# A hybrid encoder layer with a dense PEER stage: the building of the gate matrix tied to u tiles, VectorE making the low parts, and top-k positions compared in pairs

## The chip, the cores and the metric

The kernel runs on one core of a Trainium2 chip. The metric is the device time of the whole kernel in microseconds; the median of three runs stands for it. Its engines are PE (TensorE), DVE (VectorE), ACT (ScalarE), POOL (GpSimd) and SP (SyncE, which here only issues transfers). SPq and ACTq in a row are the transfer queues that SP and ACT issue. All matrix products of the big stages take 32-bit numbers as a high part `hi` (rounded) and a low part `lo` (the rest), as three products hi·hi, lo·hi, hi·lo.

## What is computed

The layer has 512 tokens of width 1024 (and 16 meta tokens in the first half). Its first half, attention, a gated linear recurrence and their projection, is not touched. The second half is PEER: each token picks, for each of 8 heads, 16 of 128·128 single-neuron experts by two lists of 128 keys.

```python
q = (xi @ w_q).reshape(n, PEER_HEADS, 2, PEER_KEY_DIM)
s = jnp.einsum('nhpc,hpkc->nhpk', q, sub_keys)
ts, ti = lax.top_k(s, PEER_TOPK)                      # 16 of 128, for each of the two lists
cand_s = ts[:, :, 0, :, None] + ts[:, :, 1, None, :]  # 256 sums
cand_i = ti[:, :, 0, :, None] * PEER_NKEYS + ti[:, :, 1, None, :]
best_s, best_p = lax.top_k(cand_s, PEER_TOPK)         # the 16 best pairs
idx = jnp.take_along_axis(cand_i, best_p, axis=-1)
gate = jax.nn.softmax(best_s, axis=-1)
act = jax.nn.gelu(jnp.einsum('nd,nhkd->nhk', xi, u[idx]), approximate=False)
return jnp.einsum('nhk,nhkd->nd', (gate * act), v[idx])
```

## The kernel before

The 512 tokens are four tiles t = 0 to 3 of 128. For t = 1 to 3 (384 tokens) PEER is computed densely: for each of 128 tiles of 128 experts a **u tile** gives gelu(u·x) for all 384 tokens, a matrix W holds each token's gates (zero where an expert was not picked), and a **v tile** adds (W·gelu)·v into the output. For t = 0 it is done sparsely: 256 indirect transfers on POOL (`gather`, L251) fetch rows of u and v, and DVE uses them (L265, L263).

The second half runs in these stages.

- **Scores and top 16.** PE multiplies by w_q and the keys; DVE takes the 16 best of 128 (`top16`, L183 to L187). `topk2` (L192 to L243) is the work behind it for half the heads and two token tiles: 80 candidate sums, their 16 best, the positions split into a row and a column number `rf` and `cf`, and then the key numbers by comparing each position with 0 to 15 (L231), multiplying with the list `tf` (L233) and folding 16 terms to one (L234 to L237). An Exp on ACT and a division (L240 to L243) give the gates. It runs four times; the last two are the list `late`.
- **u phase** (the first `LA` = 60 u tiles). A u tile loads `raw` (SP, L108, two buffers), makes `hi` on ACT (L114) and `lo` on POOL (L116; on DVE for tiles from 60 on), then 24 matmuls (L127 to L129), a gelu on ACT (L1055), and a spill to memory, `A_d` (L1057, issued by ACT). Beside it `wbuild` makes W. For a token tile, PE transposes the gates and the two key numbers (`sel`, L974) and ACT copies them out; then, for 8 tokens at a time (a step; 48 steps), DVE compares the two key numbers with `ioh` (L993, twice), multiplies the first one-hot by the gates' low part `gl` (L994) and high part `gh` (L996; every fourth step ACT does the latter, L999), PE multiplies (L1021, L1022: 8 matmuls for a bank of 4 tokens, two banks in a step), ACT copies the bank into `stg` (L1024), and every four steps SP writes `stg` to memory, `W_d` (L1026). I call the banks W0 to W95 and the tiles U0 to U127, V0 to V127. Sixteen gathers of u rows are issued in this phase (`RA` = 0.4 for each u tile).
- **v phase.** 128 v tiles with 18 matmuls each (L1080 to L1084) and, from U59 on, the remaining u tiles between them, whose gelu is not spilled. SP loads W and the spilled gelus four tiles at a time (`wa`, L1111 and L1113), and `vraw`. The other gathers are issued here.

The order of each engine's queue is set when the program is built, by a scheduler that follows a simulated timeline; the program's own order and explicit dependencies (`add_manual_dep`) steer it. In the main loop `wbuild` is advanced by a budget: after u tile i it may have used the share (i + 1)/(LA − ET − 1) of the whole cost, with a guessed cost for each piece (3.0, 4.0, 2.2 behind `yield`).

Ahead of the u phase, the tile `iof` (the numbers 0 to 127, from which `ioh` is made, L949 and L950) lies in memory that the stage before has to leave first.

Of the kernel before, what the change touches and what calls it, by code (L numbers as in the profile page):

```python
# [9 lines left out]
F32 = mybir.dt.float32  # L10
# [14 lines left out]
P = 128  # L25
# [24 lines left out]
SC = 16  # L50
# [29 lines left out]
PU = 100  # L80


def _emit(ctx, tc, I, out):
# [71 lines left out]
    io16 = cst.tile([P, TOPK], F32, name="io16")  # L155

# [32 lines left out]
    def topk2(a, b, sm, cand, tf, eq, zs):  # L189
        ts_ = tsv[:, b, 2 * a:2 * a + 2].rearrange("p t h c r -> p (t h) c r")  # L190
        ti_ = tiv[:, b, 2 * a:2 * a + 2].rearrange("p t h c r -> p (t h) c r")
        nc.vector.tensor_copy(tf, ti_)  # L192
# [25 lines left out]
        cf = sm("cf")  # L218
        nc.vector.tensor_copy(rf, row)
# [141 lines left out]
    nc.sync.dma_start(out=io16, in_=I["iota"][:, :TOPK].to_broadcast([P, TOPK]))  # L361
    ropc = fx("ropc", [P, TM], "ropc")
# [532 lines left out]

    keys = qs.tile([P, 2 * PH, NK], F32, name="keys")
# [371 lines left out]
```

## Time and profile before

| what | us |
|---|---|
| median of three runs | 1678.58 (1675.06 to 1680.83) |
| profiled run, its own time | 1682.47 |
| span of the profiled run | 1680.7 |
| first matmul of U0 | 466.21 |
| first matmul of W0 | 566.74 |
| end of the last matmul of W95 | 814.2 |
| first matmul of V0 | 846.18 |

In the page's list of busy time PE has 1574.4 us (94% of the span), DVE 1291.4 (77%), ACT 739.6 (44%), POOL 677.1 (40%). These shares are means over stages with different limits: between 500 and 850 us, which is where the u phase lies, PE is idle for about a sixth of the time. A row of the waits says for whom an engine sat idle before an instruction, for how long in total, how often, and the longest.

### The profile page before, as it was taken

The page shows a single profiled execution, that of the slowest core. Times are in us where ns is not written, and L with a number is a line of the kernel's source. Part 1 is how long each engine was busy: PE and PEld are TensorE (multiplying, and loading weights), DVE is VectorE, ACT ScalarE, POOL GpSimd, SP SyncE. Part 2 cuts the span into 40 slices and gives each one's busy share as a digit, 9 for nine tenths or more (in the row PEclk, how much of TensorE's full clock was granted, in tenths as well). Part 3 has the DMA queues.
Part 4 walks back from the last instruction along what each step waited for, and adds up shares of the span by engine and source line. Part 5 has one row for each costly group of instructions (what it writes and reads, how often), then busy time and mean ns, then how long its engine had stood idle before and what let it go on. Part 6 is the DMA issues. An engine that isn't in the chain of part 4 may idle for free.

```text
span 1680.7 us, 24243 instructions
## 1 busy us (share of the span) xinstructions
PE 1574.4 (94%) x8793; PEld 1392.4 (83%) x8793; DVE 1291.4 (77%) x2529; ACT 739.6 (44%) x1229; POOL 677.1 (40%) x465
## 2 busy tenths in 40 slices
PE   6999998989986789979989999999999999999998
PEld 6888886768876689878978888889999999988996
DVE  3888768647999998948247777778887888778777
ACT  5454555543324474867533333333333333333334
POOL 3443112076334467475411212154545444344442
PEclk9999999989997989999999999999999999999999
DMA  6112222232224557656999999899999998999885
GB/s 232 54 46 81 69 61 69 84 118 89 78 73 149 176 193 250 239 218 252 328 366 342 326 314 326 278 313 389 321 329 326 336 327 315 319 339 327 308 276 185
DMA packets 152360, 387.42 MB, mean 231 GB/s; under 512 B 12752, under 2 KB 71376, under 8 KB 150576
## 3 DMA queue, kind: packets, MB, share of 16 engines
q1 hardware_dynamic: 106160, 238.79, 41.2%
q0 software_dynamic: 36864, 134.23, 22.8%
q10 hardware_dynamic: 9216, 12.85, 2.1%
q8 instruction: 69, 1.13, 0.3%
q14 instruction: 51, 0.42, 0.1%
HBM read 342.56 MB, written 40.63 MB: 228 GB/s over the span
## 4 chain that ended last, share of the span: by engine, by line
PE 28%; issue 18%; DVE 12%; POOL 10%; DMA 6%; ACT 3%; SPq 1%; POOLq 0%; ACTq 0%; DVEq 0%
POOL gat L251 7%; PE banka L1080 4%; PE banka L1083 4%; PE banka L1084 4%; POOL lo L116 3%; PE bankp L1080 2%; PE bankp L1083 2%; PE bankp L1084 2%; PE bankg L129 2%; DMA gat<-v,idx 2%; PE bankg L127 2%; PE bankg L128 2%; DMA raw<-uT 2%; DVE oh L993 2%; DMA gat<-u,idx 1%
## 5 line engine op out<-in xcount | busy, mean ns | idle before, releaser
L116 POOL TENSOR_TENSOR lo<-raw,hi 128x1024 fp32r<-128x1024 f32 x81 | 238.4, 2947 | 228.8 <-ACT hi L114 220.4
L114 ACT CAST hi<-raw 128x1024 fp32r<-128x1024 f32 x177 | 185.8, 1051 | 289.6 <-PE bankg L128 159.1
L127 PE MATMUL bankg<-un_hi,hi 128*128 128x384 f32 x880 | 300.1, 341 | 12.2 <-ACT act L1055 12.2
L129 PE MATMUL bankg<-un_hi,lo 128*128 128x384 f32 x880 | 299.6, 341 | 5.3 <-POOL lo L116 5.2
L128 PE MATMUL bankg<-un_lo,hi 128*128 128x384 f32 x880 | 297.9, 338 | 0.0
L251 POOL DMA_INDIRECT gat<-u,idx x128 | 157.8, 1232 | 299.5 <-PE bankp L1084 252.1
L251 POOL DMA_INDIRECT gat<-v,idx x128 | 167.8, 1311 | 207.6 <-PE bankp L1084 180.4
L263 DVE SCALAR_TENSOR_TENSOR acc<-gat,sact,acc 128x1024 f32<-128x1024 f32 x128 | 164.2, 1283 | 72.2 <-DMA gat<-v,idx 61.6
L265 DVE CUSTOM_DVE_ANT_0 gat<-gat,hn 128x1024 f32<-128x1024 f32 x128 | 162.9, 1282 | 53.2 <-DMA gat<-u,idx 53.1
L127 PEld LDWEIGHTS bankg<-un_hi,hi 128*128 128x128 f32 x880 | 168.1, 191 | 16.1 <-ACT act L1055 12.5
L135 DVE TENSOR_TENSOR vhl<-vraw,vhl 128x1024 fp32r<-128x1024 f32 x128 | 157.1, 1228 | 30.9 <-ACT vhl L134 30.8
L129 PEld LDWEIGHTS bankg<-un_hi,lo 128*128 128x128 f32 x880 | 167.9, 191 | 8.1 <-POOL lo L116 6.8
L128 PEld LDWEIGHTS bankg<-un_lo,hi 128*128 128x128 f32 x880 | 167.7, 191 | 3.4
L134 ACT CAST vhl<-vraw 128x1024 fp32r<-128x1024 f32 x128 | 134.2, 1049 | 46.3 <-PE bankp L1084 33.4
L116 DVE TENSOR_TENSOR lo<-raw,hi 128x1024 fp32r<-128x1024 f32 x96 | 117.8, 1228 | 24.2 <-ACT hi L114 23.0
L1024 ACT ACTIVATE stg<-banka 128x512 f32<-128x512 f32 x96 | 96.2, 1140 | 1.7 <-PE banka L1022 0.9
L993 DVE TENSOR_TENSOR oh<-iT,ioh 128x1024 f16<-128x1024 f16 x96 | 80.8, 888 | 2.4 <-PE banka L1022 2.4
L1021 PE MATMUL banka<-oh 128*128 128x128 f16 x384 | 55.3, 233 | 22.1 <-DVE oh L996 12.7
L1055 ACT ACTIVATE act<-bankg 128x384 f32<-128x384 f32 x110 | 53.4, 486 | 23.2 <-PE bankg L129 12.1
L1021 PEld LDWEIGHTS <-oh 128*128 128x128 f16 x384 | 39.2, 104 | 20.8 <-DVE oh L996 15.0
L1022 PE MATMUL banka<-oh 128*128 128x128 f16 x384 | 54.3, 233 | 0.7 <-DVE oh L994 0.7
L129 PE MATMUL bankp<-un_hi,lo 128*128 128x384 f32 x144 | 48.7, 338 | 4.5 <-POOL lo L116 4.5
(2283 smaller groups left out, 3906.3 us busy)
## 6 DMA issues: line engine op xcount, KB each, us to landing
raw<-uT SPq DMA_DIRECT2D x128, 512.0 KB
vraw<-v SPq DMA_DIRECT2D x128, 512.0 KB
W_d<-stg SPq DMA_DIRECT2D x12, 2048.0 KB
wa<-W_d SPq DMA_DIRECT2D x32, 768.0 KB
A_d<-act ACTq DMA_DIRECT2D x60, 192.0 KB
wa<-A_d SPq DMA_DIRECT2D x15, 768.0 KB
raw<-wq SPq DMA_DIRECT2D x16, 512.0 KB
raw<-win_n SPq DMA_DIRECT2D x12, 512.0 KB
```

The source lines that it names most:

```text
L114: nc.scalar.copy(hi, raw)
L116: (eng or nc.vector).tensor_sub(lo, raw, hi.bitcast(F32))
L127: nc.tensor.matmul(o, lhsT=ah, rhs=bh, start=start, stop=False)
L128: nc.tensor.matmul(o, lhsT=ah, rhs=bl, start=False, stop=False)
L129: return nc.tensor.matmul(o, lhsT=al, rhs=bh, start=False, stop=stop)
L134: last[0] = nc.scalar.copy(hi, src).ins.name
L135: (eng or nc.vector).tensor_sub(lo, src, hi.bitcast(F32))
L251: g = nc.gpsimd.indirect_dma_start(out=r, out_offset=None, in_=src, in_offset=bass.IndirectOffsetOnAxis(ap=idx[:, hk:hk + 1], axis=0))
L263: nc.vector.scalar_tensor_tensor(acc0, r, sact[:, hk:hk + 1], acc0, op0=ALU.mult, op1=ALU.add)
L265: nc.vector.tensor_tensor_reduce(r, r, hn0, scale=1.0, scalar=0.0, op0=ALU.mult, op1=ALU.add, accum_out=sact[:, hk:hk + 1])
L993: nc.vector.tensor_tensor(o12[:, j], tok(iT[:, j]), ioh[:, None, :, :].to_broadcast(sh), op=ALU.is_equal)
L1080: m0 = nc.tensor.matmul(o, lhsT=gh_[:, tc_], rhs=vh[:, dc], start=(j == 0), stop=False, skip_group_check=True)
```

## The change

1. **W is tied to u tiles.** The budget is gone. Step n of `wbuild` belongs to u tile `tgt(n)` = 15 + int(0.48·n), 10 more from n = 14 on; the first matmul of a step and the transposes are tied (order only) behind the last matmul of that u tile. The steps of t = 1 without the last two start at U15, the rest at U31.
2. **Gates later.** `topk2` no longer ends with Exp and division; they are the function `fin`, called for two at a time, its Exp tied behind the gelu of u tile 13 and of u tile 30.
3. **Low parts on VectorE.** `LP` = 8: POOL makes `lo` for U0 to U7 only; DVE makes it for the rest.
4. **Pairs.** Positions `rb`, `cb` are bf16; `tf` and the numbers 0 to 15 (`io16b`) hold each entry twice, so that two positions lie side by side and every operand of the comparison is 16 bits wide with adjacent elements. The fold has 3 adds and a last one for each list, as before.
5. **One-hots in one piece.** The two comparisons of a step are one instruction on 128x2048; the two multiplications also, except in each fourth step.
6. `iof` has a place of its own and is loaded ahead of the keys.
7. `W_d` is written from ACT's queue instead of SP's.
8. `RA` 0.4 → 0.15 (5 gathers in the u phase in place of 16), `LA` 60 → 56 (4 u tiles move into the v phase), `SC` 16 → 14 (buffers of the scores).

```diff
-SC = 16
+SC = 14
-RA = 0.4
+RA = 0.15
-LA = 60
+LA = 56
-PU = 100
+LP = 8
+A0 = 15
+AR = 0.48
+AG = 10
+AL = 14
...
-        nc.vector.tensor_copy(tf, ti_)
+        nc.vector.tensor_copy(tf, ti_[:, :, :, :, None].to_broadcast([P, PH, 2, TOPK, 2]))
...
-        for j, pos in enumerate((rf, cf)):
-            nc.vector.tensor_tensor(eq, pos[:, :, :, None].to_broadcast([P, PH, TOPK, TOPK]),
-                                    io16[:, None, None, :].to_broadcast([P, PH, TOPK, TOPK]), op=ALU.is_equal)
...
-        nc.scalar.activation(gate, gate, AF.Exp)
...
+        for j, pos in enumerate((rb, cb)):
+            e4 = eq
+            nc.vector.tensor_tensor(e4.rearrange("p g (r q) -> p g r q", q=2),
+                                    pos.rearrange("p h (s q) -> p (h s) q", q=2)[:, :, None, :].to_broadcast([P, PH * 8, TOPK, 2]),
+                                    io16b[:, None].to_broadcast([P, PH * 8, TOPK, 2]), op=ALU.is_equal)
...
+            for w in (16, 8, 4):
+                nc.vector.tensor_add(e4[:, :, :w], e4[:, :, :w], e4[:, :, w:2 * w])
...
+        def fin(at):
+            e = nc.scalar.activation(gate, gate, AF.Exp)
+            tc.add_manual_dep(e.ins, gelus[at], ORDER_DEP, reason="order")
...
+    iof = w1.tile([P, NK], F32, name="iof")
+    nc.sync.dma_start(out=iof, in_=I["iota"].to_broadcast([P, NK]))
     keys = qs.tile([P, 2 * PH, NK], F32, name="keys")
...
+        def tgt(n):
+            return A0 + int(n * AR) + (AG if n >= AL else 0)
...
-            for j in range(2):
-                nc.vector.tensor_tensor(o12[:, j], tok(iT[:, j]), ioh[:, None, :, :].to_broadcast(sh), op=ALU.is_equal)
-            nc.vector.tensor_mul(ol, o12[:, 0], tok(gl))
-            if m0 // OB % DM < DN:
-                nc.vector.tensor_mul(od, o12[:, 0], tok(gh))
+            nc.vector.tensor_tensor(o12, tok(iT[:, blk].rearrange("p j m -> p (j m)")),
+                                    ioh[:, None, :, :].to_broadcast([P, 2 * GQ, NK, QI]), op=ALU.is_equal)
...
+                    if g_ + q2 == 0:
+                        tc.add_manual_dep(m.ins, anchors[tgt(n)], ORDER_DEP, reason="order")
...
-                nc.sync.dma_start(out=W_d[:, ((t - 1) * P + m0) // BL], in_=stg)
+                nc.scalar.dma_start(out=W_d[:, ((t - 1) * P + m0) // BL], in_=stg)
...
-            U[i] = stream(I["uT"][i], eng=nc.gpsimd if i < LA and i % PU != PU - 1 else None)
+            U[i] = stream(I["uT"][i], eng=nc.gpsimd if i < LP else None)
```

What the scheduler makes of it is seen at three places. On PE, the first transposes (they read `sel`, the gates and key numbers of t = 1) stood one by one inside U7, U10 and U13. Before, inside U7:

```order
L127 MATMUL bankg<-un_hi,hi 128x384
L128 MATMUL bankg<-un_lo,hi 128x384
L129 MATMUL bankg<-un_hi,lo 128x384
L974 MATMUL bankp<-ident,sel 128x128
L127 MATMUL bankg<-un_hi,hi 128x384
```

And after the change, where all three stand together:

```order
L131 MATMUL bankg<-un_hi,hi 128x384
L132 MATMUL bankg<-un_lo,hi 128x384
L133 MATMUL bankg<-un_hi,lo 128x384
L996 MATMUL bankp<-ident,sel 128x128 x3
L131 MATMUL bankg<-un_hi,hi 128x384
```

The three now stand between U15 and U16; U0 to U15 run without anything between them, and W0 stands inside U19 where it stood inside U15.

On DVE, the rest of `topk2` for the first two token tiles held no low part. Before, around the first comparison of the second group of heads:

```order
L226 TENSOR_TENSOR sm_cf<-sm_cf,sm_t_4416 128x128
L228 TENSOR_TENSOR sm_rf<-sm_rf,sm_t_4416 128x128
L185 MATCH_REPLACE sc<-tsv,sc 128x128 x4
L231 TENSOR_TENSOR eq<-sm_rf,io_75 128x2048
L186 MAX tsv<-sc 128x8 x3
```

After the change, around the first low part of the u phase, which is that of U8:

```order
L190 MATCH_REPLACE cand<-sm_bsv,cand 128x80 x2
L239 TENSOR_TENSOR eq<-sm_rb,io16b 128x2048
L191 MAX sm_bsv<-cand 128x8 x3
L120 TENSOR_TENSOR lo<-raw,hi 128x1024
L192 MAX_INDEX sm_bp<-sm_bsv,cand 128x8
L191 MAX sm_bsv<-cand 128x8
L192 MAX_INDEX sm_bp<-sm_bsv,cand 128x8
L191 MAX sm_bsv<-cand 128x8 x2
L243 TENSOR_TENSOR eq<-eq,tf 128x2048
```

`lo` of U8 has moved into DVE's queue, behind all of top16 and behind the second 16-of-80 search of the same token tiles (`cand`), and the low parts of U9 and on follow a few rows apart.

Later on DVE, in the steps of W (`oh` is the one-hot, `iT` the key numbers, `gs` the two parts of the gates). Before:

```order
L993 TENSOR_TENSOR oh<-iT,ioh 128x1024 x2
L994 TENSOR_TENSOR oh<-oh,gl 128x1024
L996 TENSOR_TENSOR oh<-oh,gh 128x1024
L993 TENSOR_TENSOR oh<-iT,ioh 128x1024 x3
L994 TENSOR_TENSOR oh<-oh,gl 128x1024
L996 TENSOR_TENSOR oh<-oh,gh 128x1024
```

After:

```order
L1018 TENSOR_TENSOR oh<-iT,ioh 128x2048 x2
L1023 TENSOR_TENSOR oh<-oh,gs 128x2048
L120 TENSOR_TENSOR lo<-raw,hi 128x1024
L1023 TENSOR_TENSOR oh<-oh,gs 128x2048
L1018 TENSOR_TENSOR oh<-iT,ioh 128x2048 x2
L120 TENSOR_TENSOR lo<-raw,hi 128x1024
```

Each step has two long instructions in place of four short ones, and a low part stands after each two or three of them. On PE the banks W32 to W95 lie between U35 and U49 after the change, and between U32 and U52 before it.

## Rows read from the trace of the kernel before

**Rows 1.** Busy time of the engines in stretches of 50 us; PEclk is the granted clock, then the transfer engines' busy share and rate.

```profile
500.00:550.00 50.00, 30.49 (x151) 28.84 (x151) 47.65 (x228) 18.52 (x23) 19.95 (x8) 0.77 0.41 138
...
800.00:850.00 50.00, 41.97 (x269) 40.22 (x268) 13.55 (x16) 24.18 (x37) 16.52 (x7) 0.94 0.96 347
```

**Rows 2.** What PE waited for from 500 to 850 us: total, times, longest.

```profile
PE banka L1021 <- DVE oh L996: 12.7, 9, 3.4
PE bankg L127 <- ACT act L1055: 12.2, 1, 12.2
PE banka L1021 <- ACT stg L1024: 9.3, 9, 3.7
PE bankp L974 <- DVE sel L237: 8.0, 2, 5.5
...
PE bankp L974 <- DVE sel L243: 5.1, 1, 5.1
```

**Rows 3.** What SP's queue waited for from 400 to 850 us.

```profile
SPq L1026 <- ACT stg L1024: 26.0, 10, 8.2
SPq L949 <- DVE tiv L187: 21.3, 1, 21.3
```

**Rows 4.** ACT's timeline: `hi` of U7, with its wait in brackets.

```profile
507.34 1.04 ACT L114 CAST hi<-raw 128x1024 fp32r<-128x1024 f32 x1 [21.80 <-DMA raw<-uT]
```

**Rows 5.** PE's timeline: first matmul of U0, last of U6, first of U7, first of W0, two of W95, first of V0.

```profile
466.21 0.44 PE L127 MATMUL bankp<-un_hi,hi 128*128 128x384 f32 x1
...
496.33 0.34 PE L129 MATMUL bankg<-un_hi,lo 128*128 128x384 f32 x1
...
508.82 0.69 PE L127 MATMUL bankg<-un_hi,hi 128*128 128x384 f32 x1 [12.16 <-ACT act L1055]
...
566.74 0.28 PE L1021 MATMUL banka<-oh 128*128 128x128 f16 x2 [0.96 <-DVE oh L996]
...
813.90 0.22 PE L1022 MATMUL banka<-oh 128*128 128x128 f16 x1
813.96 0.22 PE L1021 MATMUL banka<-oh 128*128 128x128 f16 x1
...
846.18 0.79 PE L1080 MATMUL banka<-vhl,gh__8527 128*128 128x512 f32 x1 [6.92 <-ACT gh__8527 L134]
```

**Rows 6.** DVE's timeline behind top16: the search in the 80 candidates begins, the wait for `iof`, and the first comparison of positions after it.

```profile
501.58 1.26 DVE L183 MAX8 sm_bsv<-cand 128x8 f32<-128x80 f32 x8
...
506.13 0.29 DVE L950 CAST ioh<-iof 128x256 f16<-128x256 f32 x1 [2.23 <-DMA iof<-iota]
...
521.92 2.28 DVE L231 TENSOR_TENSOR eq<-sm_rf,io 128x2048 bf16<-128x2048 f32 x1
```

**Rows 7.** The same instruction's form with 16-bit operands on the whole of 128x2048: shortest, median and longest of 8, in ns.

```profile
L233 DVE TENSOR_TENSOR eq<-eq,tf x8: 1211/1270/3301, 462.4 to 642.9; 128x2048 bf16<-128x2048 bf16 x8
```

**Rows 8.** Groups of instructions from 540 to 820 us, by form: count, busy us, mean ns, idle before.

```profile
L116 POOL TENSOR_TENSOR lo<-raw,hi 128x1024 fp32r<-128x1024 f32 x43 | 146.2, 3406 | 97.7 <-ACT hi L114 89.4 <-PE banka L1022 8.2
L1024 ACT ACTIVATE stg<-banka 128x512 f32<-128x512 f32 x96 | 96.2, 1140 | 1.7 <-PE banka L1022 0.9 <-ACT act L1055 0.8
L993 DVE TENSOR_TENSOR oh<-iT,ioh 128x1024 f16<-128x1024 f16 x96 | 80.8, 888 | 2.4 <-PE banka L1022 2.4
...
L994 DVE TENSOR_TENSOR oh<-oh,gl 128x1024 f16<-128x1024 f16 x48 | 43.4, 908 | 0.0
...
L996 DVE TENSOR_TENSOR oh<-oh,gh 128x1024 f16<-128x1024 f16 x36 | 33.2, 924 | 0.0
```

**Rows 9.** DVE's timeline: two multiplications of the same form, one after the other.

```profile
568.36 0.68 DVE L994 TENSOR_TENSOR oh<-oh,gl 128x1024 f16<-128x1024 f16 x1
...
569.57 2.88 DVE L994 TENSOR_TENSOR oh<-oh,gl 128x1024 f16<-128x1024 f16 x1
```

**Rows 10.** POOL's timeline at that place: a low part.

```profile
568.99 2.91 POOL L116 TENSOR_TENSOR lo<-raw,hi 128x1024 fp32r<-128x1024 f32 x1 [4.48 <-ACT hi L114]
```

**Rows 11.** A packed stretch of ACT's timeline: the eight pieces of L999, a cast, a gelu, copies of banks.

```profile
688.52 2.49 ACT L999 ACTIVATE oh<-oh,gT 128x128 f16<-128x128 f16 x8 [3.10 <-DVE oh L993]
690.88 1.03 ACT L114 CAST hi<-raw 128x1024 fp32r<-128x1024 f32 x1
691.82 0.48 ACT L1055 ACTIVATE act<-bankg 128x384 f32<-128x384 f32 x1
...
693.03 3.01 ACT L1024 ACTIVATE stg<-banka 128x512 f32<-128x512 f32 x3
695.83 1.07 ACT L114 CAST hi<-raw 128x1024 fp32r<-128x1024 f32 x1
```

**Rows 12.** A low part of the same size where DVE makes it (whole run): count, busy us, mean ns, idle before.

```profile
L116 DVE TENSOR_TENSOR lo<-raw,hi 128x1024 fp32r<-128x1024 f32 x96 | 117.8, 1228 | 24.2 <-ACT hi L114 23.0
```

**Rows 13.** The chain that ended last, from W95 to V0: start, us, what.

```profile
815.51 1.20 ACT stg L1024
816.73 8.12 DMA W_d<-stg
...
835.05 10.12 DMA vraw<-v
```

**Rows 14.** A stretch of the v phase, columns as in Rows 1.

```profile
1000.00:1200.00 200.00, 200.00 (x941) 172.67 (x940) 160.69 (x238) 72.91 (x101) 73.36 (x58) 1.00 0.93 323
```

**Rows 15.** POOL's timeline: the last gather.

```profile
1653.70 1.30 POOL L251 DMA_INDIRECT gat<-v,idx  x1 [0.30 <-issue]
```

More of the change, by code (lines that the diff above doesn't have):

```diff
@@ L155, in _emit @@
     io16 = cst.tile([P, TOPK], F32, name="io16")
+    io16b = cst.tile([P, TOPK, 2], BF, name="io16b")
     def half(name, tag, j, n):
@@ L247, in _emit @@
+        def fin(at):
+            e = nc.scalar.activation(gate, gate, AF.Exp)
+            tc.add_manual_dep(e.ins, gelus[at], ORDER_DEP, reason="order")
+            nc.vector.tensor_reduce(zs, gate, axis=AX.X, op=ALU.add)
+            nc.vector.reciprocal(zs, zs)
+            nc.vector.tensor_mul(dst(0), th(gate), th(zs[:, :, None].to_broadcast([P, PH, TOPK])))
+        fins.append(fin)
+    anchors, gelus, fins = [], [], []
     GB = 32
@@ L973, in prep @@
                 for j in range(3):
-                    nc.tensor.transpose(out=tr[:, j, :], in_=sel[:, j, t].rearrange("p h r -> p (h r)"), identity=ident)
+                    m = nc.tensor.transpose(out=tr[:, j, :], in_=sel[:, j, t].rearrange("p h r -> p (h r)"), identity=ident)
+                    tc.add_manual_dep(m.ins, anchors[at], ORDER_DEP, reason="order")
                 gT = wk2.tile([P, P], F32, name="gT")
                 nc.scalar.activation(gT, tr[:, 0, :], AF.Copy, scale=GS)
-                iT = wk2.tile([P, 2, P], F16, name="iT")
@@ new lines, in prep @@
+                nc.scalar.copy(iT.rearrange("p b j m -> p j b m"), tr[:, 1:3, :].rearrange("p j (b m) -> p j b m", m=OB))
+                gs = wk2.tile([P, P // OB, 2, OB], F16, name="gs")
+                g8 = gT.rearrange("p (b m) -> p b m", m=OB)
+                nc.vector.tensor_copy(gs[:, :, 0, :], g8)
+                nc.vector.tensor_sub(gs[:, :, 1, :], g8, gs[:, :, 0, :])
+                cur[t] = gT, iT, gs
+            gT, iT, gs = cur[t]
+            GQ = OB // QI
+            sh = [P, GQ, NK, QI]
@@ L1020, in wbuild @@
                     w_ = o12[:, 1, m_[0], :, m_[1]]
[L1021 removed]
+                    m = nc.tensor.matmul(b[:, q2, :], lhsT=w_, rhs=od[:, m_[0], :, m_[1]], start=True, stop=False)
+                    if g_ + q2 == 0:
+                        tc.add_manual_dep(m.ins, anchors[tgt(n)], ORDER_DEP, reason="order")
                     nc.tensor.matmul(b[:, q2, :], lhsT=w_, rhs=ol[:, m_[0], :, m_[1]], start=False, stop=True)
@@ L1116, in _emit @@
     wb = wbuild()
-    cost = done = 0.0
-    total = 3.0 * 5 * len(tks) + 40.0 + C1 + 48 * 2.2
+    due = next(wb)
     u_split(0)
@@ L1123, in _emit @@
         u_split(i + 2)
-        while done < total * (i + 1) / (LA - ET - 1):
-            c = next(wb, None)
-            if c is None:
-                break
-            done += c
+        while due <= i:
+            due = next(wb, NK)
         if i == LA - ET:
```

76 lines of the change are left out of this document (38 added, 38 removed).

## Prediction

> **What bounds the kernel now.** I read the stretches of 50 us first, then PE's waits in the u phase, then what stands behind the longest of them. In the v phase PE is busy for 200.00 of 200 us at a granted clock of 1.00, with the transfer engines at 0.93 [rows 14]: a v phase with unchanged content keeps its length, and a u tile moved into it costs its matmuls. The u phase is different: PE has 30.49 us of work between 500 and 550, at a mean clock of 0.77, and 41.97 between 800 and 850 [rows 1]. So the time to be had lies between U0 (466.21) and V0 (846.18), 380 us [rows 5].
>
> How much of it is work? U0 to U6 take 466.21 to 496.67, with four short matmuls among them [rows 5]: (496.67 − 466.21)/7 = 4.35, and 24 matmuls at the 0.173 us by which they follow each other are 4.2 us; I take 4.2 for a u tile at full clock. In W95 one matmul starts 0.06 after the other (813.90, 813.96) [rows 5], so a bank of eight is 0.46. Before: 59 tiles × 4.2 + 96 banks × 0.46 = 248 + 44 = 292 us. The other 88 are waits and half clock. The five largest waits are 12.7 + 12.2 + 9.3 + 8.0 + 5.1 = 47.3 [rows 2], and the stretch from W95 to V0 has one of 6.92 [rows 5]. The 12.2 is one event: SP's queue stands for 21.3 us at `iof` [rows 3], U7's `raw` is behind it, ACT waits 21.80 for that [rows 4], PE 12.16 for ACT [rows 5]. The 8.0 and 5.1 are transposes that stood in PE's queue ahead of u tiles whose operands were there.
>
> **The change part by part.**
>
> *`iof` early, and U7.* SP's queue no longer stops, U7 follows U6, and PE finishes the eight tiles with POOL's low parts at about 466.2 + 8 × 4.3 = 500.7. DVE's `ioh` cast no longer waits 2.23 [rows 6].
>
> *The low part of U8.* It now stands in DVE's queue behind top16, a 16-of-80 search and the first paired comparison. DVE is busy for 47.65 of 50 us there [rows 1]. Before, that stretch ran from 501.58 to the comparison at 521.92 [rows 6], 20.3 us. Off go the wait of 2.23, about 2.1 of collisions with POOL's three low parts, and 0.5 of gate work that is now in `fin`: 15.5. The start, 501.6, gains 2.2 from two earlier comparisons and loses 0.8 to the longer `tf`; I leave it between 500.2 and 502. Then the comparison (1.21) and some searches (0.4), and the low part itself (1.23, [rows 12]): PE can go on at 518.5 to 520. So the waits of 12.2 and 5.1 go and one of **17.6 to 19** comes in their place; I take 18. It is queue order and not load: PE stands for it with nothing else to do, because the transposes and W are now tied behind U15. What is late next is the low part of U9, which has 4.2 us of PE behind it and some 4 us of DVE rows. The transposes between U15 and U16 find `sel` ready long before (the two waits of 5.5 and 2.5 go). W0 then starts at about 466.2 + 19.6 × 4.2 + 18 + 5 for half clock behind the wait = 571, where it was at 566.74 [rows 5], but with 19.6 tiles done instead of 15.7: four tiles, 16 us, ahead.
>
> *The comparison in pairs.* With a 32-bit position it takes 2.28 [rows 6]; the same size with 16-bit operands takes 1.21 at best, 1.27 in the median [rows 7]. Eight comparisons save 8 × 1.07 = 8.6 us of DVE, of which only the early two lie on the path just told. The bounds: nothing, if pairs with a repeated operand run as the 32-bit form does, and 8.6 if as rows 7. I take rows 7, since `tf` is read with a repeat there too.
>
> *Low parts on DVE.* POOL made 43 of them from 540 to 820 in 3406 ns each; the one-hot work took 888, 908 and 924 ns beside it [rows 8], against 0.68 alone, and a neighbour took 2.88 while POOL's ran from 568.99 to 571.90 [rows 9, 10]. The excess is 96 × 0.21 + 48 × 0.23 + 36 × 0.24 = 40 us of DVE's time; 43 × 1.23 = 53 us come onto it. So DVE carries 13 us more in 280 and PE is rid of its waits for POOL. The trace shows the mechanism as a stop of about 2.2 us, not as a slower rate. The Trainium skill has a rule for that (SBUF — State Buffer, Who interferes with whom): an operation of VectorE with two SBUF inputs and a GpSimd operation that reads SBUF exclude each other for a whole instruction. The trace agrees in kind (2.88 against 0.68). By it alone each of 43 low parts could have cost DVE its whole length, 146 us in all; the 40 us of the rows are what I use.
>
> *One-hots in one piece.* The step had four instructions of 0.68 and has two of 1.21, or 1.21 + 0.68: 2.7 to 2.4, nearly nothing. They are gates for PE, though: a bank now waits for all of it. WL keeps one step of lead, which is the cover; without it the price would be 1.2 a step.
>
> *W32 to W95, the second part.* It lies between U35 and U49, 14 tiles. **PE**: 14.3 × 4.2 + 64 × 0.46 = 60 + 29 = 90, or 85 with the tighter 0.173 and tile fractions. **DVE**: 32 × 1.21 + 24 × 1.21 + 8 × 0.68 + 14 × 1.23 + three uses of a gather at 1.2 (an estimate, by rows 12) = 38.7 + 29.0 + 5.4 + 17.2 + 3.6 = 94. **ACT**: three copies and the start of the next instruction are 695.83 − 693.03 = 2.80, so 64 × 0.93 = 59.7; a cast and a gelu take 0.94 + 0.38, × 15 = 19.8; the eight pieces 690.88 − 688.52 = 2.36, × 8 = 18.9 [rows 11]; and 3.5 for the rest: **102**. So ScalarE becomes the bound of this part, 17 us beyond PE at the least; and since ACT's eight pieces wait for DVE and its queue is in order, I allow up to 118.
>
> *The first part, W0 to W31*, holds 13.4 tiles and 32 banks: 71 us of PE, 62 of ACT, DVE just in time with `late`'s top-k and `fin` among it. I take 76. Then U33 to U35, 12.
>
> *W_d on ACT's queue.* SP stood 26.0 us for `stg` [rows 3], in front of `raw`; that goes. An issue costs ACT some 0.3 us × 12. The Trainium skill (DMA: Bandwidth & Descriptors, Issuing engines are not separate DMA queues) has it that this saves issue time only, since the same transfer engines do the work. By it this part would be worth nothing; the row shows the gain to be the order of SP's queue, so far as PE waits for `raw`, which it hardly does: nothing in the sum.
>
> *V0.* From 571: 571 + 76 + 12 = 659, + 102 to 118 = 761 to 777 for W95. V0 came 32 us behind W95, since the rest of the u tiles, the last `W_d` (8.12) and `vraw` (10.12) lie there [rows 13]; five or six tiles lie there still. V0 at 793 to 809, **801**. That is 45 before 846.2.
>
> *v phase.* Four more u tiles there: + 4 × 4.2 = 16.8. Eleven gathers more are some 5.8 MB, with the tiles 8 MB, in a phase longer by 2%: the transfer engines stay near 0.93 [rows 14]. The gathers end later against PE; the last was issued at 1653.70 [rows 15], and I allow + 2.5 (0 to 6). `SC` at 14 lies under DVE's continuous top16: nothing; if not, 2 us.
>
> *Sum.* −45.2 + 16.8 + 2.5 = −25.9. The profiled run took 1682.47, 3.9 above the median, so 1682.5 − 25.9 − 3.9 = 1652.7, **1653**.
>
> **The rivals.**
>
> *A. ACT and DVE keep up.* Then W32 to W95 take 85 to 90: V0 at 776 to 784, −64 + 19 = −45, **1634**. For it: PE's waits for `stg` were 9.3 us in all of the phase [rows 2], so that ACT as a bound is a sum of mine. Against it: the 102 are pitches of packed work, with nothing left to gain.
>
> *B. The saving is given back.* The low parts of U9 to U18 come late as that of U8 does, because their rows on DVE stand between searches, and the one-hots of t = 1 come late behind them; or the u phase ends in a chain through `W_d` and `vraw` that doesn't shrink. 25 us of new waits: V0 at 826, **1678**.
>
> *C. VectorE becomes the bound: slower.* The long one-hots have more dimensions with repeats than the short ones. If they ran as the 32-bit form does, 2.28 in place of 1.21 [rows 6, 7], 48 + 36 of them would cost 84 × 1.07 = 90 us more. DVE's load from W0 to W95 would be some 160 + 90 = 250 in the 200 that the forecast gives them, and V0 would come at about 855: + 9 + 19 = + 28, **1707**. It decides as soon as a long one-hot takes more than 1.7 us. Rows 7 speak against it, at the same size with a repeated operand.
>
> *D. It doesn't do what it says.* The ties hold in the printed order; low parts leave POOL. What could fail is the purpose: the stall of U7 only moves to U8, and if nothing else is won, −16 of work ahead stays as it is against 17 in the v phase: about **1680**.
>
> **How the numbers follow.** A measurement of this kernel can tell about 0.3% from no change, 5 us: faster is below 1673.5, slower above 1683.6. The forecast gets 0.50 (1643 to 1668 by its own bounds of V0 and the tail), A 0.17, B 0.18 (half of it below 1673.5), C 0.09, D 0.06 (half of it slower at most 1684). Faster: 0.50 + 0.17 + 0.09 + 0.01 = 0.77; same: 0.09 + 0.03 = 0.12; slower: 0.09 + 0.02 = 0.11. The range takes in A and B: 1632 to 1680.
>
> **What would show it.** Right: SP without a stop at `iof`; PE standing once, 17 to 19 us, ahead of U8, for DVE's low part; W0 near 571 inside U19; from W32 to W95 ACT busy for over 90% of the time and PE waiting for `stg` or for the one-hot that ACT makes; long one-hots at 1.2 us; V0 near 801. Wrong: PE's waits there for DVE's one-hots and low parts (B or C), a long one-hot beyond 1.7 (C), PE without a gap (A), or a v phase longer by much more than 17 us, which would be the gathers or the transfers.

## The result, and the profile after

| | before | after |
|---|---|---|
| median, us | 1676.82 (1668.81 to 1680.83, 4 runs) | 1650.42 (1648.02 to 1652.2, 4 runs) |
| profiled run, its own time / span | 1682.47 / 1680.7 | 1648.02 / 1646.2 |
| U0 | 466.21 | 470.03 |
| W0, after U0 | 100.5 | 103.8 |
| W0 to the end of W95 | 247.5 | 184.0 |
| V0, after U0 | 380.0 | 323.0 |
| V0 to the end of the span | 834.5 | 853.2 |

The ratio is 0.9848, with a 95% interval of 0.9808 to 0.9887: 26.4 us of the median, where the sum had 25.9. The two profiled runs lie at opposite ends of their runs, so that their spans are 34.5 apart: some 8 us of that is how executions differ, and not the change. U0 comes between 464.4 and 472.5 in the traces of this study, early and late ones among kernels with the change; so I compare times after U0. V0 is 57 us sooner after U0, and the rest 18.7 longer.

PE's timeline of the kernel after: first matmul of U0, the first behind the wait in U8, W0, V0.

```profile
470.03 0.44 PE L131 MATMUL bankp<-un_hi,hi 128*128 128x384 f32 x1
...
522.36 0.69 PE L133 MATMUL bankp<-un_hi,lo 128*128 128x384 f32 x1 [17.39 <-DVE lo L120]
...
573.83 0.24 PE L1054 MATMUL banka<-oh 128*128 128x128 f16 x1
...
793.02 0.79 PE L1113 MATMUL banka<-vhl,gh__8281 128*128 128x512 f32 x1 [9.53 <-ACT gh__8281 L138]
```

All that PE waited for in the u phase, 466 to 830 us:

```profile
PE bankp L133 <- DVE lo L120: 17.4, 1, 17.4
PE banka L1113 <- ACT gh__8281 L138: 9.5, 1, 9.5
PE banka L1054 <- ACT stg L1059: 8.1, 15, 2.2
PE bankg L133 <- DVE lo L120: 1.4, 2, 1.2
PE banka L1054 <- DVE oh L1018: 0.8, 1, 0.8
PE banka L1054 <- DVE oh L1023: 0.7, 1, 0.7
```

Two rows of the kernel before that [rows 2] leaves out, its waits for POOL's low parts:

```profile
PE bankg L129 <- POOL lo L116: 5.2, 3, 3.9
...
PE bankp L129 <- POOL lo L116: 4.5, 1, 4.5
```

These waits are gone after the change, and so are those for transposes and for U7 of [rows 2]. The waits for one-hots shrank from 12.7 to 1.5. The longest wait that is left is the forecast one ahead of U8's low part (the bracket stands at its third matmul, the first that needs `lo`).

Busy time before, from W0 to W32 and on to the end of W95, columns as in [rows 1]:

```profile
566.70:672.80 106.10, 92.56 (x661) 89.16 (x661) 99.41 (x101) 64.39 (x102) 70.53 (x23) 0.94 0.61 220
672.80:814.10 141.30, 124.20 (x1010) 117.90 (x1010) 103.21 (x131) 106.67 (x168) 79.36 (x29) 0.96 0.67 243
```

Busy time after, columns as in [rows 1], from W0 to W32, to the end of W95, to V0, and in a stretch of the v phase (compare [rows 14]):

```profile
573.80:659.30 85.50, 83.61 (x649) 81.63 (x647) 70.82 (x86) 67.33 (x102) 11.77 (x2) 1.00 0.71 252
659.30:757.90 98.60, 89.46 (x834) 84.36 (x834) 78.04 (x76) 91.36 (x144) 5.38 (x2) 1.00 0.70 255
757.90:793.00 35.10, 25.33 (x143) 24.34 (x142) 9.83 (x12) 13.14 (x18) 0.00 (x0) 0.92 0.92 324
...
1000.00:1200.00 200.00, 200.00 (x981) 177.81 (x980) 162.14 (x239) 73.09 (x101) 92.37 (x67) 1.00 0.93 332
```

The columns behind the length are PE, weight loads, DVE, ACT and POOL. In the first part PE is busy for 83.61 of 85.50 us. In the second ACT is, for 91.36 of 98.60 (93%), and PE for 89.46. The granted clock is 1.00 in both; before, it was 0.94 and 0.96.

The groups of the W work after, from 540 to 800 us, answer to [rows 8]:

```profile
L1059 ACT ACTIVATE stg<-banka 128x512 f32<-128x512 f32 x96 | 97.8, 1151 | 10.3 <-PE banka L1057 6.9 <-ACT act L1088 1.7 <-ACT stg L1059 1.4
...
L1018 DVE TENSOR_TENSOR oh<-iT,ioh 128x2048 f16<-128x2048 f16 x48 | 56.8, 1218 | 1.1 <-PE banka L1057 0.9
L120 DVE TENSOR_TENSOR lo<-raw,hi 128x1024 fp32r<-128x1024 f32 x42 | 51.2, 1221 | 48.5 <-ACT hi L118 48.4
...
L1023 DVE TENSOR_TENSOR oh<-oh,gs 128x2048 f16<-128x2048 f16 x36 | 43.0, 1218 | 0.0
```

One instruction of 1218 ns compares two key numbers, where two of 888 did before. Nothing stops DVE in these any more: the shortest of the 48 took 1212 ns and the longest 1226.

### The profile page after: what moved, and what is told of

Same layout as the page of the kernel before. It is cut to its first block, busy times and chain, and to the rows that moved or that the text cites. A ratio compares the mean times of both kernels' runs of the same rounds, so it can differ in the third digit from the quotient of the medians.

```text
span 1646.2 us, 24113 instructions
## 1 busy us (share of the span) xinstructions
PE 1566.2 (95%) x8793; PEld 1385.3 (84%) x8793; DVE 1261.1 (77%) x2498; ACT 739.3 (45%) x1227; POOL 520.9 (32%) x413
## 4 chain that ended last, share of the span: by engine, by line
PE 51%; DVE 9%; issue 5%; ACT 5%; DMA 5%; POOL 2%; SPq 1%; ACTq 0%; POOLq 0%; DVEq 0%
PE banka L1113 6%; PE banka L1116 6%; PE banka L1117 6%; PE bankg L133 6%; PE bankg L131 6%; PE bankg L132 6%; ACT stg L1059 3%; PE bankp L1113 3%; PE bankp L1116 3%; PE bankp L1117 3%; DMA gat<-v,idx 3%; POOL gat L264 2%; PE banka L131 1%; PE banka L132 1%; PE banka L133 1%
## 5 line engine op out<-in xcount | busy, mean ns | idle before, releaser
L264 POOL DMA_INDIRECT gat<-u,idx x128 | 172.4, 1347 | 584.8 <-PE bankp L1117 254.4
L120 DVE TENSOR_TENSOR lo<-raw,hi 128x1024 fp32r<-128x1024 f32 x148 | 180.7, 1222 | 74.5 <-ACT hi L118 73.7
L264 POOL DMA_INDIRECT gat<-v,idx x128 | 162.9, 1273 | 203.9 <-PE bankp L1117 176.9
L278 DVE CUSTOM_DVE_ANT_0 gat<-gat,hn 128x1024 f32<-128x1024 f32 x128 | 154.5, 1219 | 21.5 <-DMA gat<-u,idx 21.3
L139 DVE TENSOR_TENSOR vhl<-vraw,vhl 128x1024 fp32r<-128x1024 f32 x128 | 156.1, 1220 | 11.7 <-ACT vhl L138 10.4
L120 POOL TENSOR_TENSOR lo<-raw,hi 128x1024 fp32r<-128x1024 f32 x29 | 70.7, 2438 | 67.1 <-ACT hi L118 67.0
L1088 ACT ACTIVATE act<-bankg 128x384 f32<-128x384 f32 x112 | 54.5, 487 | 24.5 <-PE bankg L133 12.2
L133 PE MATMUL bankp<-un_hi,lo 128*128 128x384 f32 x128 | 44.4, 347 | 17.4 <-DVE lo L120 17.4
L1054 PE MATMUL banka<-oh 128*128 128x128 f16 x384 | 49.3, 219 | 9.9 <-ACT stg L1059 8.1
L1018 DVE TENSOR_TENSOR oh<-iT,ioh 128x2048 f16<-128x2048 f16 x48 | 56.8, 1218 | 1.1 <-PE banka L1057 0.9
L131 PE MATMUL banka<-hg_hi,hi 128*128 128x512 f32 x128 | 52.0, 406 | 0.0
L132 PE MATMUL banka<-hg_lo,hi 128*128 128x512 f32 x128 | 51.2, 400 | 0.0
```

Source lines behind the costliest of these rows:

```text
L120: (eng or nc.vector).tensor_sub(lo, raw, hi.bitcast(F32))
L131: nc.tensor.matmul(o, lhsT=ah, rhs=bh, start=start, stop=False)
L132: nc.tensor.matmul(o, lhsT=ah, rhs=bl, start=False, stop=False)
L133: return nc.tensor.matmul(o, lhsT=al, rhs=bh, start=False, stop=stop)
L139: (eng or nc.vector).tensor_sub(lo, src, hi.bitcast(F32))
L264: g = nc.gpsimd.indirect_dma_start(out=r, out_offset=None, in_=src, in_offset=bass.IndirectOffsetOnAxis(ap=idx[:, hk:hk + 1], axis=0))
```

## The experiments

Times are from each kernel's profiled run, in us; the ratio is to the kernel before on the same chip.

| kernel | W0 − U0 | W0 to W95 | V0 − U0 | V0 to end | ratio (95%) |
|---|---|---|---|---|---|
| before | 100.5 | 247.5 | 380.0 | 834.5 | 1 |
| after | 103.8 | 184.0 | 323.0 | 853.2 | 0.9848 (0.9808 to 0.9887) |
| e1_lp12 | 106.0 | 186.0 | 327.7 | 859.7 | 0.9833 (0.9781 to 0.9886) |
| e2_dn4 | 103.1 | 182.8 | 318.9 | 851.4 | 0.9744 (0.9691 to 0.9796) |
| e4_lp56 | 96.6 | 213.5 | 343.5 | 862.4 | 0.9946 (0.9911 to 0.9980) |
| e5_lp12_a19 | 122.1 | 174.3 | 332.1 | 853.5 | 0.9879 (0.9826 to 0.9932) |
| f1_lp18_dn4 | 100.1 | 185.8 | 318.7 | 852.0 | 0.9757 (0.9668 to 0.9846) |
| f2_lp22_dn4_a18 | 112.4 | 171.4 | 315.7 | 851.5 | 0.9744 (0.9677 to 0.9812) |
| b0_iof | 98.0 | 243.2 | 373.4 | 830.9 | 0.9994 (0.9964 to 1.0024) |
| b1_lp8 | 107.8 | 231.4 | 372.3 | 834.3 | 0.9922 (0.9891 to 0.9953) |
| a_ra4 | 102.2 | 198.1 | 332.1 | 850.6 | 0.9798 (0.9778 to 0.9818) |
| a_f32pos | 103.7 | 184.8 | 323.5 | 855.0 | 0.9820 (0.9799 to 0.9842) |
| e3_wd_sp | 103.1 | 184.1 | 321.1 | 856.6 | 0.9768 (0.9738 to 0.9799) |
| a_la60 | 103.1 | 185.8 | 329.6 | 861.5 | 0.9887 (0.9860 to 0.9914) |

**Is the wait ahead of U8 what it costs?** e1_lp12, on the kernel after:

```diff
-LP = 8
+LP = 12
```

> POOL makes the low parts of U8 to U11 too; nothing else changes in the order. Theory: the 17.4 us for which PE stands ahead of U8 is a place in VectorE's queue, but it is not what sets W0. Behind it VectorE's own chain (the 16-of-80 search, the paired comparisons, the gates' division, then the one-hots) goes on at its own pace: the transposes find the gates ready only 3.5 us ahead of PE. So the wait ahead of U8 shrinks to under 3 us, and 8 to 12 us of it come back as a wait of the transposes or of W0 for VectorE; the span is 2 to 7 us shorter than that of the changed kernel (1646), no more. Rival: the 17.4 us are simply lost, and about 14 us of them come back: span 1630 to 1634.

Neither came. PE's timeline in e1_lp12:

```profile
538.29 0.69 PE L133 MATMUL bankg<-un_hi,lo 128*128 128x384 f32 x1 [19.58 <-DVE lo L120]
```

The wait moved to U12 and grew to 19.6 us: the scheduler put the first low part that is DVE's still further back, behind both key numbers of the group of heads that stood ahead of it. So the place of the wait follows the border between POOL's and DVE's low parts. Its price is open after this run. e5_lp12_a19 has that border and the first part of W four u tiles later:

```diff
-LP = 8
-A0 = 15
+LP = 12
+A0 = 19
...
-AG = 10
+AG = 6
```

> As the run with POOL's low parts up to U11, and the transposes and steps of the first token tile tied four u tiles later (19 in place of 15), the second part where it was. Theory (VectorE's chain to the gates is what W0 waits for, and PE can fill the time with u tiles): PE has no wait over 4 us from U0 to W0, W0 comes within 3 us of the changed kernel's 573.8 but with four tiles more done, W32 comes 8 to 14 us sooner, and so does V0: span 1632 to 1639. Rival (ScalarE and VectorE are the pace through the whole of the W work): W32 and V0 move by less than 4 us.

Wrong for the same reason: the wait of 19.6 stands at U12 again, and W0 is 18 us later after U0. W0 to W95 takes only 174.3, with four u tiles fewer in it, and V0 is 9 us later.

**Does ScalarE set the pace of the second part?** e2_dn4:

```diff
-DN = 3
+DN = 4
```

> VectorE makes the high product of every fourth step too, in one instruction of 1.2 us with the low one, so that ScalarE loses its eight pieces (12 x 2.4 us, 19 of them between W32 and W95) and VectorE gets 12 x 0.55 us. Theory (ScalarE sets the pace from W32 to W95, 93% busy there): that stretch, 98.7 us in the changed kernel, comes to 88 to 92, PE's own content is the next bound, and the span is 6 to 10 us shorter. Rival (PE's order or VectorE sets it): the stretch stays within 3 us and the span too.

Busy time in e2_dn4 from W32 to the end of W95:

```profile
663.10:756.10 93.00, 92.89 (x871) 89.81 (x870) 84.21 (x78) 81.76 (x94) 2.96 (x2) 1.00 0.79 288
```

The stretch went from 98.6 to 93.0. ACT, rid of its pieces, is busy for 81.76 of it, where it was for 91.36, and PE for 92.89: PE has no wait left there. So ACT was the bound, and PE is the next one, 5.6 us behind. V0 is 4 us sooner after U0; the forecast length of 88 to 92 was 1 us short.

**What do low parts on VectorE do?** e4_lp56 gives all of them in the u phase back to POOL:

```diff
-LP = 8
+LP = 56
```

> All low parts of the u phase go back to POOL, the rest of the change stays. Theory: low parts on VectorE are no gain by load (53 us of its own against 40 us of stops that POOL's cause), and they bring the wait ahead of U8; what they buy is that PE doesn't wait for POOL and one-hots come evenly. Going back takes the 17.4 us ahead of U8 away, brings stops of 2.2 us into VectorE's chain up to the gates, some 8 of them, and puts one-hots of W at 0.4 to 0.6 us more each: W0 within 5 us, the stretch from W32 to W95 5 to 15 us longer, span 0 to 15 us longer than 1646. Rival: the stops fall where nothing waits for VectorE, and the span is over 5 us shorter.

The sign of the theory held, its size didn't: W0 came 7 us sooner after U0, W0 to W95 took 29.5 us more, V0 is 20.5 later, and the ratio 1% worse. e4_lp56's groups from 540 to 800 us:

```profile
L120 POOL TENSOR_TENSOR lo<-raw,hi 128x1024 fp32r<-128x1024 f32 x36 | 123.6, 3437 | 101.7 <-ACT hi L118 96.7 <-PE bankp L133 4.6
L1018 DVE TENSOR_TENSOR oh<-iT,ioh 128x2048 f16<-128x2048 f16 x48 | 80.8, 1714 | 0.1
...
L1023 DVE TENSOR_TENSOR oh<-oh,gs 128x2048 f16<-128x2048 f16 x36 | 49.3, 1395 | 0.0
...
L1029 ACT ACTIVATE oh<-oh,gT 128x128 f16<-128x128 f16 x96 | 29.9, 430 | 15.7 <-DVE oh L1018 14.0 <-DVE oh L1023 0.4 <-ACT stg L1059 0.4
```

On the one-hots the stops are 48 × 0.50 + 36 × 0.18 = 30 us of DVE's time, less than the 44 us that 36 low parts of 1.22 cost it. ACT waits 14.0 us for these one-hots, ahead of its eight pieces, with copies of banks behind them in its queue. But stops go both ways. PE's waits in e4_lp56:

```profile
PE bankp L996 <- DVE sel L255: 15.1, 1, 15.1
PE banka L1054 <- ACT stg L1059: 13.0, 29, 2.6
PE bankp L133 <- POOL lo L120: 10.8, 1, 10.8
PE banka L1054 <- DVE oh L1023: 7.6, 5, 3.3
```

The 10.8 us belong to one low part on POOL, which took 22.18 us while DVE worked without a gap until 608.6:

```profile
588.65 22.18 POOL L120 TENSOR_TENSOR lo<-raw,hi 128x1024 fp32r<-128x1024 f32 x1 [6.09 <-ACT hi L118]
```

```profile
610.89 0.69 PE L133 MATMUL bankp<-un_hi,lo 128*128 128x384 f32 x1 [10.82 <-POOL lo L120]
```

The next gather stands behind low parts in POOL's queue, so that DVE in turn waits for rows, 39.2 us in place of 4.4:

```profile
DVE gat L278 <- DMA gat<-u,idx: 39.2, 3, 19.7
```

From W0 to W95 PE waits 20.6 us more than in the kernel after: 10.8 for that one low part, 6.1 for one-hots and 4.9 for copies of banks (less 1.2 for a low part on DVE); and it is busy 8.6 us longer, at a granted clock of 0.95 and 0.97 instead of 1.00. So the run shows what low parts on POOL cost, but the stops of one-hots are only a part of it, and which part no run separates.

b1_lp8 makes that part of the change alone, on the kernel before:

```diff
-PU = 100
+LP = 8
...
-            U[i] = stream(I["uT"][i], eng=nc.gpsimd if i < LA and i % PU != PU - 1 else None)
+            U[i] = stream(I["uT"][i], eng=nc.gpsimd if i < LP else None)
```

> The kernel before with one part of the change: low parts from U8 on by VectorE, all else as before, the budget too. Theory: the stops of VectorE by POOL go (40 us of its time) and 53 us of its own come; PE's waits for POOL (about 10 us in the u phase) go, and the wait ahead of the first low part of VectorE comes, 5 to 15 us beyond what PE waits for the gates there anyway: V0 0 to 12 us sooner, which the tail gives back by nothing; span 1670 to 1682. Rival (low parts on VectorE are the main gain of the change): V0 25 us sooner or more.

V0 is 7.7 us sooner, as expected, and the ratio is 0.9922 (10 runs), half of what the whole change brings. With the rest of the change the same edit is worth 20.5 us at V0 (e4_lp56).

**What is ahead of W0?** f1_lp18_dn4 moves the border to U18, behind which no wait for the chain can hide:

```diff
-LP = 8
-DN = 3
+LP = 18
+DN = 4
```

> Of the changed kernel: POOL makes the low parts of U0 to U17, and VectorE the high products of every fourth step. In the run with POOL up to U11 the wait of 17.4 us had not gone but moved to U12 (19.6 us), since the first low part that is VectorE's was put behind the whole chain to the gates. Theory: with the border at U18 no u tile ahead of W0 stands behind that chain; PE runs from U0 to U15 without a wait and then waits 8 to 15 us at the transposes; the gates are ready 3 to 8 us sooner (seven low parts of 1.2 us off VectorE's chain, some stops of 2 us onto it). W0 comes 95 to 99 us after U0 (103.8 in the changed kernel, 96.6 with all low parts on POOL), V0 309 to 315 us after U0 (323.0; 318.9 with the products alone on VectorE); span 1629 to 1638. Rival (ScalarE's and VectorE's load from W0 on is the pace, a start of W sooner only waits there): V0 at 317 to 320 us after U0.

PE's waits in f1_lp18_dn4, 466 to 850 us:

```profile
PE bankp L996 <- DVE sel L255: 13.9, 1, 13.9
PE banka L1113 <- ACT gh__8185 L138: 10.2, 1, 10.2
PE bankg L133 <- DVE lo L120: 4.8, 1, 4.8
```

PE ran to U15 without a wait, and then waited 13.9 us at the transposes. W0 came 3 us sooner after U0 than in e2_dn4, and V0 0.2: the rival. So the 17.4 us ahead of U8 are not lost as such.

The kernel after shows why: the gates (L255) come ready, and then PE gets to the transposes.

```profile
553.45 0.49 DVE L253 TENSOR_REDUCE zs<-sm_gate 128x8 f32<-128x128 f32 x2 [0.79 <-ACT sm_gate L251]
...
554.09 0.48 DVE L255 TENSOR_TENSOR sel<-sm_gate,zs 128x128 f32<-128x128 f32 x2
```

```profile
558.06 0.49 PE L996 MATMUL bankp<-ident,sel 128*128 128x128 f32 x3
```

The gates are ready at 554.57, only 3.5 us ahead of PE. DVE even waits a little there, for the Exp that is tied behind U13's gelu and with it behind PE's own wait. In f1_lp18_dn4 the Exp was done 21 us sooner after U0, and no low part of the u phase stood in DVE's chain; yet the gates were ready 81.7 us after U0, where it was 84.5:

```profile
549.75 0.48 DVE L255 TENSOR_TENSOR sel<-sm_gate,zs 128x128 f32<-128x128 f32 x2
```

So DVE's chain from top16 to the gates holds W0 back almost as long as PE's wait does: PE has time to spare on the way, and the wait only takes up a part of it. f2_lp22_dn4_a18 fills the spare time:

```diff
-LP = 8
-A0 = 15
-AG = 10
-DN = 3
+LP = 22
+A0 = 18
+AG = 7
+DN = 4
```

> As the run before, with POOL's low parts up to U21 and the first transposes and steps tied three u tiles later (18 in place of 15; the second part where it was). Theory: PE fills what was its wait at the transposes with U16 to U18, waits under 4 us there, W0 comes 96 to 101 us after U0 with three more u tiles done, and 8 to 13 us of it are left at V0: 298 to 307 us after U0, span 1618 to 1629. Rival (the first part is paced by VectorE: with the second top-k of the late token tiles between the one-hots it can't be packed into fewer u tiles): V0 within 4 us of the run before.

V0 is 3 us sooner after U0 than in f1_lp18_dn4, near the rival. PE's wait at the transposes fell to 6.0, W0 has over three more u tiles behind it, and the second part began 10.4 us sooner after U0; but it took 101.3 us in place of 93.0. DVE's timeline there, POOL's gather, and the wait of PE that follows:

```profile
669.13 2.35 DVE L1018 TENSOR_TENSOR oh<-iT,ioh 128x2048 f16<-128x2048 f16 x2
679.03 1.23 DVE L278 CUSTOM_DVE_ANT_0 gat<-gat,hn 128x1024 f32<-128x1024 f32 x1 [7.55 <-DMA gat<-u,idx]
```

```profile
661.29 11.01 POOL L264 DMA_INDIRECT gat<-u,idx  x1 [32.78 <-DVE oh L1018]
```

```profile
682.59 0.29 PE L1054 MATMUL banka<-oh 128*128 128x128 f16 x1 [4.75 <-DVE oh L1023]
```

The use of a gathered row stands in DVE's queue between one-hots, and the rows were 7.55 us late. POOL's instruction for the gather took 11.01 us, beside a DVE that worked without a gap until 671.48, and ended 0.8 us behind that; the one-hot behind the use then held PE for 4.75. With e2_dn4 it has the best ratio of all, 0.9744; the two can't be told apart.

**iof alone.** b0_iof, on the kernel before, with SC = 14 for the room:

```diff
+    iof = w1.tile([P, NK], F32, name="iof")
+    nc.sync.dma_start(out=iof, in_=I["iota"].to_broadcast([P, NK]))
     keys = qs.tile([P, 2 * PH, NK], F32, name="keys")
...
-    iof = wk.tile([P, NK], F32, name="iof")
-    nc.sync.dma_start(out=iof, in_=I["iota"].to_broadcast([P, NK]))
```

> The kernel before with one part of the change: the numbers 0 to 127 have a place of their own and are loaded ahead of the keys (with 14 score buffers, which makes the room). Theory: SP's stop of 21.3 us and ACT's wait of 21.8 go, but PE's 12.2 don't come back, since the transpose of the gates inside U7 is next in PE's order and finds its gates 2 us sooner at most: PE waits 16 to 21 us there, U8 starts 0 to 4 us sooner after U0, span 0 to 5 us shorter. Rival (the 12.2 us are worth what the row says): U8 and V0 10 to 12 us sooner.

The longest wait of PE in b0_iof:

```profile
PE bankp L974 <- DVE sel L243: 18.4, 1, 18.4
```

As expected: the 12.2 us of U7 and the 5.1 behind them became one wait at the transpose, W0 is 2.5 us sooner, and the ratio is 0.9994. V0 is 6.6 sooner in this one trace, 4 of it between W0 and W95; the ten runs don't show it.

**Gathers, the comparison, W_d, LA.** Four runs on the kernel after.

```diff
-RA = 0.15
+RA = 0.4
```

> The changed kernel with 16 gathers in the u phase again instead of 5. Theory (a gather in the u phase is paid by VectorE's order: its use stands between one-hots and waits for the rows to land, 35.8 us in the kernel before for 16, 4.4 us for 5 in the changed one, and each use takes 1.2): W0 to W95, 184.0 us in the changed kernel, gets 8 to 25 us longer, the tail gives back 2; span 5 to 20 us longer. Rival (VectorE has room there, 71 of 85 and 78 of 99 us busy, so the gathers cost nothing): within 4 us.

W0 to W95 is 14.1 us longer, as the theory had it, and DVE's uses wait for rows for 22.2 us (4.4 after):

```profile
DVE gat L278 <- DMA gat<-u,idx: 22.2, 6, 6.3
```

V0 is 9.1 us later, 2.6 come back behind it, and the span of the trace is 3.7 longer. In the whole the theory's 5 to 20 us don't show: the median is 1648.6, where a_f32pos below, which up to V0 runs as the kernel after does, has 1650.3 on the same chip. So the stretch bears the theory out, and the whole time the rival.

```diff
-        rb = sm("rb", BF)
-        cb = sm("cb", BF)
+        rb = sm("rb")
+        cb = sm("cb")
```

(and `io16b` in 32 bits)

> The changed kernel with positions and the list 0 to 15 in 32 bits, compared in the same pairs. Theory: the comparison takes 2.2 to 2.3 us in place of 1.22; two of them lie ahead of U8's low part, two more ahead of the gates of t = 1, so that PE's wait ahead of U8 is 2 us longer and W0 comes 2 to 5 us later after U0 than 103.8; the other four lie beside PE work; V0 2 to 6 us later, span 0 to 6 us longer. Rival (32-bit operands in pairs run at the faster rate too): 1.2 us and no difference.

The comparison by `rb`, in ns: shortest, median, longest of four.

```profile
L239 DVE TENSOR_TENSOR eq<-sm_rb,io16b x4: 2272/2278/2283, 461.3 to 565.9; 128x2048 bf16<-128x2048 f32 x4
```

The rate is as forecast (1216 with 16 bits), but it is worth nothing: W0 and V0 stay within 0.5 of the kernel after, where 2 to 6 us were expected. The order isn't quite the same: U8's low part was put ahead of the comparison by `rb` in DVE's queue this time, and PE's wait there was 15.9.

```diff
-                nc.scalar.dma_start(out=W_d[:, ((t - 1) * P + m0) // BL], in_=stg)
+                nc.sync.dma_start(out=W_d[:, ((t - 1) * P + m0) // BL], in_=stg)
```

> The changed kernel with W_d written from SP's queue again. Theory: SP's queue waits for the copies of banks ahead of raw loads, 20 to 30 us in all, but PE has its low parts two tiles ahead, so that V0 stays within 3 us and the span within 4. Rival (raw loads behind W_d come late): PE waits 8 us or more for hi or lo between W0 and W95, and the span is over 6 us longer.

SP's queue waits for the copies of banks for 73.4 us, more than the 20 to 30 expected, and yet W0 to W95 is 184.1:

```profile
SPq L1061 <- ACT stg L1059: 73.4, 11, 11.1
```

So ACT's queue brings nothing. It may cost a little: the median here is 1643.7, against 1650.3 of a_f32pos on the same chip; the trace doesn't show where that would come from.

```diff
-LA = 56
+LA = 60
```

> The changed kernel with 60 u tiles ahead of the v phase again. Theory: the four tiles cost PE their matmuls wherever they stand: V0 comes 15 to 18 us later after U0 than 323.0 and the rest is 15 to 18 us shorter than 853.2, span within 4 us of the changed kernel's. Rival (they fill the stretch from W95 to V0, where PE waits 9.5 us for the first v tiles): V0 only 7 to 11 us later and the span 6 to 9 us shorter.

Both wrong. V0 is 6.6 later after U0, since the scheduler put three of the four tiles among V1 to V5; and the rest got 8.3 us longer instead of 17 shorter. POOL's last gather, DVE's last use of one, and PE's last matmul, in a_la60 (span 1660.6):

```profile
1636.36 1.36 POOL L264 DMA_INDIRECT gat<-v,idx  x1 [0.30 <-issue]
```

```profile
1644.06 1.28 DVE L276 SCALAR_TENSOR_TENSOR acc<-gat,sact,acc 128x1024 f32<-128x1024 f32 x1 [0.49 <-DMA gat<-v,idx]
```

```profile
1645.98 0.39 PE L1117 MATMUL bankp<-vhl,gl__15134 128*128 128x512 f32 x1
```

The gathers end it: from PE's last matmul to the end of the span it takes 14.2 us, and 7.2 in the kernel after, which is 7 of the 8.3. By the program's own rates (RA a u tile from U12 to six before LA; 0.85 a v tile from V4 on, 2.85 from V(LA) on) there is place for 258 gathers before, 255 after, and 247 here: nine of 256 are left behind the last v tile. So LA = 56 goes with RA = 0.15: with LA = 56 four more v tiles have the higher rate, which makes place for the gathers that left the u phase.

## Why the prediction was right, and where it wasn't

- **The time** was forecast as 1653 and came as 1650.4. That it is so near is luck in part. V0 after U0 was forecast as 334.8 and came at 323.0; the rest was to be 19.3 longer and was 18.7. So the traces gained 12 us more than the sum. U0 came 3.8 later, and the other 8 are the opposite ends at which the two profiled runs lie.
- **U0 to W0.** Forecast 571 − 466.2 = 104.8 after U0, measured 103.8, with 19.7 tiles done (19.6 forecast). The wait ahead of U8 is 17.4 (17.6 to 19). But "PE stands for it with nothing else to do" named the wrong cost: f1 takes that wait away and W0 gains 3 us. And `sel` was not "ready long before" the transposes, but 3.5 us. The sum came out because PE and DVE's chain to the gates get there at nearly the same time.
- **U7's 12.2** "go": they go, and b0_iof shows that alone they are worth nothing measurable.
- **Low parts.** The load was right (about 40 us of stops off, 53 on). The step took it for a cost of 13 us of DVE and no gain but PE's waits for POOL, which got no number. e4 shows 20.5 us of gain at V0. About half of PE's extra waits there is a single low part that POOL couldn't finish beside a busy DVE, and the other half one-hots and copies of banks that came late. The forecast had that gain without naming it, since the parts of W were summed for engines that don't stop each other.
- **W32 to W95.** "ScalarE becomes the bound": shown by e2_dn4. The term of 102 to 118 was mis-sized; it took 98.6, ACT busy for 91.4 of it. The 102 had all 64 copies, eight sets of pieces and 15 casts with their gelus; the stretch holds 60, seven and 13 of them, which at the same pitches is 90. The lead, "17 us beyond PE at the least" (12 by its own 90 for PE), is 5.6 by e2_dn4. This term is most of the 12 us by which V0 came sooner than forecast. The first part was forecast 76 + 12 and took 85.5. From W95 to V0 32 were taken and 35 came, with the last `W_d` in the chain as forecast (8.26), and a load of `raw` (10.41) where the forecast had one of `vraw`.

The chain from W95 to V0 after, as in [rows 13]:

```profile
762.92 1.06 ACT stg L1059
764.00 8.26 DMA W_d<-stg
...
781.61 10.41 DMA raw<-uT
```

- **v phase.** + 16.8 + 2.5 forecast, + 18.7 measured. a_la60 shows that the four tiles aren't simply moved content: without them the gathers don't fit.
- **Not in the sum:** eleven gathers fewer in the u phase. They shorten W0 to W95 by 14 us (a_ra4), though the whole time doesn't show it. The forecast had only the length of their uses, 1.2 each, and not the wait for the rows.
- **Costed at nothing, and so:** `W_d` (e3_wd_sp brings no loss). The pairs were costed at 2 us on the path, and a_f32pos finds nothing. Long one-hots ran at 1218 ns: rival C is out. D, that the stall only moves, is half true: it did move, and f1 prices it at 3 us of W0 and 0.2 of V0.

What stays open: no run takes out the tie of W to u tiles or the long one-hots alone, so that what is left of the 63 us between W0 and W95 beside the low parts (29.5) and the gathers (14) is not put down to a cause. And the stretch from V0 to the end varies by 12 us over the kernels with the change (850.6 to 862.4), for which only a_la60's reason is shown.

## What to carry to other kernels

A long wait in the table of an engine's waits is worth what the next thing in its queue would not have waited for anyway: ask when that was ready before costing the wait. When engines hand work on in a chain (one-hot, scaling, matmul, copy), sum each engine's work for the stretch to find the bound, and count only what lies inside the stretch. Then look at both queues of two engines that stop each other: beside the 30 us that DVE lost on one-hots in e4_lp56, one instruction of POOL took 22 us and all that stood behind it in POOL's queue came late. Work that is paced by other work, as the gathers here by tiles, has a budget: count its places before moving either.

## What the runs showed of the hardware

A low part of 128x1024 on POOL beside one-hots of 128x2048 on DVE cost each comparison 0.50 us in the mean (1714 against 1218 ns). It took 3437 ns itself in the mean, 2397 in the median where POOL makes it in the kernel after, and 22.18 us once, while DVE worked without a gap (e4_lp56). POOL's instruction for an indirect gather took 11.01 us beside such a stretch of DVE (f2_lp22_dn4_a18) and 10.46 in the kernel after, against 1.28 in the median of those of v rows there. The rows of a gather in the u phase came up to 19.7 us after DVE was ready for them (e4_lp56). A comparison of 2048 elements took 1216 ns with 16-bit operands, of which one repeats in pairs, and 2278 ns with 32-bit inputs of the same layout.
